# Contrast adjustment on one core: tiles of eight images in two slots among tiles of four in one

## The chip, the core and the metric

The kernel runs on one core of a Trainium2 chip. The metric is the device time of one execution in microseconds (us). The core's engines are named as the profile names them: PE (TensorE), DVE (VectorE), ACT (ScalarE), POOL (GpSimd) and SP (SyncE). Transfers between HBM and the on-chip memory run on 16 DMA engines; SP and ACT issue them, each on a queue of its own.

## What is computed

48 planes (16 images of 3 channels) of 512 × 512 float32 values, 1 MB each. This text calls a plane an image, as the change does. Each image is stretched about its own mean and clipped:

```python
x = rand(16, 3, 512, 512)          # float32, 50.3 MB
factor = 1.5
mean = np.mean(x, axis=(2, 3), keepdims=True)
return np.clip(mean + factor * (x - mean), 0, 1)
```

A value of the output depends on the whole image through its mean, so an image must have been read to its end before its first value can be written. With the mean folded in, an output value is factor · x + (1 − factor) · mean, clipped to 0 and 1.

## The kernel before

**Tiles.** An image is cut into 32 rows of 8,192 values (32 KB), one row to a partition, so a tile of 128 partitions holds four images, 4 MB. There are twelve tiles.

**The ring.** All data lives in one on-chip buffer, `ring`, of six slots of 32 KB per partition (line 66). Tile t uses slot t % 6. It is loaded there, changed in place and stored from there.

**Loads** are issued on SP (line 76). At the start five transfers fill the six slots: tile 0 in two parts (2,048 columns, then 6,144), tile 1, tiles 2 and 3 in one transfer, tiles 4 and 5 in one. After the computing of tile t, the load of tile t + 6 is issued (line 112); it waits until the store of tile t has landed, since it overwrites that slot. SP issues in order, so a load that waits holds up those behind it.

**Computing a tile** (lines 78 to 98). DVE adds up the first 4,352 columns of each row (line 81) while ACT adds up the other 3,840 (line 84; it writes a copy of them into `junk`, which nobody reads). Two matmuls on PE with the matrix `blockw` (lines 86, 87) add the partial sums of the 32 rows of an image, times (1 − factor)/pixels, and leave the result in `bias`, on each row of that image. The first waits for ACT's sum, the second for DVE's. Then DVE makes two passes over all 8,192 columns: times factor plus bias (line 91), and max with 0, min with 1 (line 94). `blockw` is made by POOL at the start (lines 61, 63): zeros, and four blocks of 32 × 32 with the weight.

**Stores** are issued on ACT after the second pass (line 101). The instructions of each engine stand in the order in which the program was written (`manual_schedule`): on ACT the store of tile t comes before the sum of tile t + 1, and on DVE the passes of tile t before the reduction of tile t + 1. Tile 0 is scaled and stored in two parts, of 2,048 and 6,144 columns.

Of the kernel before, what the change touches and what calls it, by code (L numbers as in the profile page):

```python
# [1 line left out]

# [4 lines left out]


P = 128  # L10
ROW = 8192
BUFS = 6
SHORT = 2048
FIRST = (SHORT, ROW - SHORT)
SUM = 4352


@with_exitstack
def kernel(
    ctx: ExitStack,  # L20
    tc: tile.TileContext,
    x: bass.AP,
    factor: float,
    out: bass.AP,
):

    nc = tc.nc
    f32 = mybir.dt.float32  # L30
    Alu = mybir.AluOpType
    Act = mybir.ActivationFunctionType

    B, C, H, W = x.shape
    n_img, n_pix = B * C, H * W
    ppi = n_pix // ROW
    per_tile = P // ppi
    n_tiles = n_img // per_tile
    assert ppi * ROW == n_pix and per_tile * n_tiles == n_img

    factor = float(factor)
    wconst = (1.0 - factor) / float(n_pix)

    x_f = x.rearrange("b c h w -> (b c h w)")
    out_f = out.rearrange("b c h w -> (b c h w)")

    def dram(ap, t, c0=0, c1=ROW):
        return bass.AP(tensor=ap.tensor, offset=t * P * ROW + c0, ap=[[ROW, P], [1, c1 - c0]])

    consts = ctx.enter_context(tc.tile_pool(name="consts", bufs=1))  # L50
    xpool = ctx.enter_context(tc.tile_pool(name="xpool", bufs=1))
    small = ctx.enter_context(tc.tile_pool(name="small", bufs=1))
    psum = ctx.enter_context(tc.tile_pool(name="psum", bufs=1, space=bass.MemoryType.PSUM))


    sums = small.tile([P, 2 * n_tiles], f32, name="sums")
    junk = small.tile([P, ROW - SUM], f32, name="junk")
    bias = psum.tile([P, n_tiles], f32, name="bias")

    blockw = consts.tile([P, P], f32, name="blockw")  # L60
    nc.gpsimd.memset(blockw, 0.0)  # L61
    for a in range(0, P, ppi):
        nc.gpsimd.memset(blockw[a : a + ppi, a : a + ppi], wconst)  # L63


    ring = xpool.tile([P, BUFS, ROW], f32, name="ring")

    def load(t, c0=0, c1=ROW, n=1):

        b = t % BUFS  # L70
        src = bass.AP(
            tensor=x_f.tensor,
            offset=t * P * ROW + c0,
            ap=[[ROW, P], [P * ROW, n], [1, c1 - c0]],
        )
        nc.sync.dma_start(out=ring[:, b : b + n, c0:c1], in_=src)  # L76

    def compute(t):
        xt = ring[:, t % BUFS, :]
        own = sums[:, 2 * t : 2 * t + 2]  # L80
        nc.vector.tensor_reduce(  # L81
            out=own[:, 0:1], in_=xt[:, 0:SUM], axis=mybir.AxisListType.X, op=Alu.add
        )
        nc.scalar.activation(out=junk, in_=xt[:, SUM:ROW], func=Act.Copy, accum_out=own[:, 1:2])  # L84
        shift = bias[:, t : t + 1]
        nc.tensor.matmul(shift, blockw, own[:, 1:2], start=True, stop=False)  # L86
        nc.tensor.matmul(shift, blockw, own[:, 0:1], start=False, stop=True)  # L87
        c = 0
        for n in FIRST if t == 0 else [ROW]:
            part = xt[:, c : c + n]  # L90
            nc.vector.tensor_scalar(  # L91
                out=part, in0=part, scalar1=factor, scalar2=shift, op0=Alu.mult, op1=Alu.add
            )
            nc.vector.tensor_scalar(  # L94
                out=part, in0=part, scalar1=0.0, scalar2=1.0, op0=Alu.max, op1=Alu.min
            )
            store(t, c, c + n)
            c += n

    def store(t, c0, c1):  # L100
        nc.scalar.dma_start(out=dram(out_f, t, c0, c1), in_=ring[:, t % BUFS, c0:c1])

    with tc.manual_schedule():
        load(0, c1=SHORT)
        load(0, c0=SHORT)
        load(1)
        load(2, n=2)
        load(4, n=2)
        for t in range(n_tiles):
            compute(t)  # L110
            if t + BUFS < n_tiles:
                load(t + BUFS)


# [1 line left out]
_INS = ['x', 'factor']  # L116
_OUTS = [((16, 3, 512, 512), 'float32')]

_NUMBERS = {'factor': 1.5}


# [26 lines left out]
```

## Time and profile before

| | us |
|---|---|
| median of the timed runs (three) | 239.27 |
| lowest and highest of them | 239.14, 239.34 |
| profiled execution, first to last instruction (the span) | 237.3 |
| DVE busy | 163.1 |
| ACT busy | 43.2 |
| PE busy | 14.1 |

The profile does not give a time for its own execution beside the span. The difference of its span from the median of the timed runs, 2.0 us, is what lies around the span.

How the lines are read. A line of groups or of the timeline names the program line (L81), the engine, the operation, output<-input, and partitions × elements. In the timeline the first two numbers are the start and the duration in us, and the bracket gives how long the engine had been idle and what ended that. SPq and ACTq stand for the issuing of transfers: the line says when a transfer is issued, not when it moves. In the DMA view, q1 is the queue that SP issues on (loads) and q10 the one that ACT issues on (stores); a queue's line gives its packets, their bytes in MB (of 1,000,000 bytes), and the time that the packets took, as a share of 16 engines over the window asked for.

The DMA rows of the page, with the size of one transfer and the median time from issue to landing:

| transfer | number | KB each | us from issue to landing |
|---|---|---|---|
| load, tile 0, first part | 1 | 1,024 | 4.8 |
| load, tile 0, second part | 1 | 3,072 | 11.7 |
| load, one tile | 7 | 4,096 | 49.7 |
| load, two tiles | 2 | 8,192 | 66.7 |
| store, tile 0, first part | 1 | 1,024 | 17.5 |
| store, tile 0, second part | 1 | 3,072 | 28.2 |
| store, one tile | 11 | 4,096 | 35.8 |

### The profile page before, as it was taken

What the parts mean: (1) busy time and instruction counts of PE and PEld (TensorE: products, weight loads), DVE (VectorE), ACT (ScalarE), POOL (GpSimd) and SP (SyncE); (2) the same over time, 40 slices, a digit from 0 to 9 for tenths busy, and PEclk for the clock granted to TensorE, in tenths of its full rate; (3) what the DMA queues carried; (4) which work ended last, traced back from release to release, by engine and by line L of the source; (5) the groups of instructions that cost most, each with busy time, mean ns of one, the idle gap of its engine ahead of it and who ended that gap; (6) DMA issues with size and microseconds to landing.
All of it is one profiled execution on the core that took longest, in us unless ns stands there. A gap on an engine that the chain in (4) does not pass through costs nothing.

```text
span 237.3 us, 285 instructions
## 1 busy us (share of the span) xinstructions
PE 14.1 (6%) x48; PEld 12.0 (5%) x48; DVE 163.1 (69%) x38; ACT 43.2 (18%) x25; POOL 0.9 (0%) x9
## 2 busy tenths in 40 slices
PE   0010010001010001010010100100100100010000
PEld 0010010001010001010010100100100100010000
DVE  0079989048989328999989898891892795687000
ACT  2050230041050023050320504101400500500000
POOL 1000000000000000000000000000000000000000
DMA  7999999999999999999999999999999999999996
GB/s 297 410 442 442 421 442 359 456 439 441 442 436 414 403 431 442 442 442 442 436 442 436 414 409 425 442 442 442 442 436 442 436 420 403 425 442 442 442 442 265
DMA packets 3712, 100.66 MB, mean 424 GB/s; under 512 B 384, under 2 KB 384, under 8 KB 384
## 3 DMA queue, kind: packets, MB, share of 16 engines
q1 hardware_dynamic: 1840, 50.33, 49.7%
q10 hardware_dynamic: 1872, 50.33, 49.2%
HBM read 50.33 MB, written 50.33 MB: 424 GB/s over the span
## 4 chain that ended last, share of the span: by engine, by line
DMA 57%; DVE 29%; another core or an unknown queue 3%; PE 1%; SPq 1%; issue 0%; DVEq 0%
DMA ring<-in_x_dram 41%; DMA out_dram<-ring 16%; DVE sums L81 10%; DVE ring L91 9%; DVE ring L94 9%; PE bias L87 1%; SPq L76 1%; DVEq L91 0%
## 5 line engine op out<-in xcount | busy, mean ns | idle before, releaser
L81 DVE TENSOR_REDUCE sums<-ring 128x1 f32<-128x4352 f32 x12 | 56.2, 4683 | 45.7 <-DMA ring<-in_x_dram 45.7
L84 ACT ACTIVATE junk<-ring 128x3840 f32<-128x3840 f32 x12 | 40.8, 3403 | 163.3 <-DMA ring<-in_x_dram 107.5
L91 DVE TENSOR_SCALAR ring<-ring,bias 128x8192 f32<-128x8192 f32 (+2 forms) x13 | 54.1, 4163 | 8.9 <-PE bias L87 7.4
L94 DVE TENSOR_SCALAR ring<-ring 128x8192 f32<-128x8192 f32 (+2 forms) x13 | 53.3, 4099 | 0.4
L86 PE MATMUL bias<-sums,blockw 128*128 128x1 f32 x24 | 7.0, 361 | 190.8 <-ACT junk L84 190.8
L86 PEld LDWEIGHTS bias<-sums,blockw 128*128 128x128 f32 x24 | 6.0, 312 | 191.7 <-ACT junk L84 175.2
L87 PE MATMUL bias<-sums,blockw 128*128 128x1 f32 x24 | 7.0, 363 | 4.3 <-DVE sums L81 3.9
L87 PEld LDWEIGHTS bias<-sums,blockw 128*128 128x128 f32 x24 | 6.0, 311 | 5.3 <-DVE sums L81 5.0
L84 ACT ACTIVATION_READ_ACCUMULATOR junk<-ring 128x1 f32 x12 | 2.2, 186 | 0.0
L84 ACT ACT_TABLE_LOAD x1 | 1.3, 1283 | 0.7 <-PEq L129 0.7
L63 POOL MEMSET blockw<- 32x32 f32 x4 | 0.5, 117 | 0.2
L61 POOL MEMSET blockw<- 128x128 f32 x1 | 0.2, 204 | 0.3 <-POOLq L129 0.3
L129 POOL MEMSET const-bfloat16-1.0<- 128x1 bf16 x1 | 0.1, 111 | 0.0
L129 POOL MEMSET const-uint8-127<- 128x1 uint8 x1 | 0.1, 111 | 0.0
L129 POOL MEMSET const-float32-1.0<- 128x1 f32 x1 | 0.1, 108 | 0.0
L129 POOL MEMSET const-float32-0.0<- 128x1 f32 x1 | 0.1, 103 | 0.2 <-issue 0.2
## 6 DMA issues: line engine op xcount, KB each, us to landing
out_dram<-ring ACTq DMA_DIRECT2D x11, 4096.0 KB, 35.8
ring<-in_x_dram SPq DMA_DIRECT2D x7, 4096.0 KB, 49.7
ring<-in_x_dram SPq DMA_DIRECT2D x2, 8192.0 KB, 66.7
ring<-in_x_dram SPq DMA_DIRECT2D x1, 3072.0 KB, 11.7
out_dram<-ring ACTq DMA_DIRECT2D x1, 3072.0 KB, 28.2
ring<-in_x_dram SPq DMA_DIRECT2D x1, 1024.0 KB, 4.8
out_dram<-ring ACTq DMA_DIRECT2D x1, 1024.0 KB, 17.5
```

What stands on the lines that cost most here:

```text
L61: nc.gpsimd.memset(blockw, 0.0)
L63: nc.gpsimd.memset(blockw[a : a + ppi, a : a + ppi], wconst)
L76: nc.sync.dma_start(out=ring[:, b : b + n, c0:c1], in_=src)
L81: nc.vector.tensor_reduce(out=own[:, 0:1], in_=xt[:, 0:SUM], axis=mybir.AxisListType.X, op=Alu.add)
L84: nc.scalar.activation(out=junk, in_=xt[:, SUM:ROW], func=Act.Copy, accum_out=own[:, 1:2])
L86: nc.tensor.matmul(shift, blockw, own[:, 1:2], start=True, stop=False)
L87: nc.tensor.matmul(shift, blockw, own[:, 0:1], start=False, stop=True)
L91: nc.vector.tensor_scalar(out=part, in0=part, scalar1=factor, scalar2=shift, op0=Alu.mult, op1=Alu.add)
L94: nc.vector.tensor_scalar(out=part, in0=part, scalar1=0.0, scalar2=1.0, op0=Alu.max, op1=Alu.min)
L129: nc = _bacc.Bacc("TRN2", target_bir_lowering=False, num_devices=1)
```

## The change

The program is written for tiles of two sizes. `PLAN` lists, for each of eight tiles, its first slot and its number of slots: (0, 1), (1, 2), (3, 2), (5, 1), and the same again. A one-slot tile is as before: four images in rows of 32 KB. A two-slot tile holds eight images, each in 16 rows of 16,384 values (64 KB), and a row lies in two neighbouring slots of its partition.

- `load` and `store` move one tile each, 4 or 8 MB. The transfers of two tiles at once are gone: at the start tile 0 is loaded in two parts, then tiles 1, 2 and 3. Tile t + 4 takes the place of tile t and is loaded after its store.
- The sums: for one slot DVE adds up 3,840 columns and ACT 2,176 twice; for two slots DVE adds up 7,552 and ACT 2,944 three times. There is one matmul for each partial sum, ACT's first and DVE's last: three for one slot, four for two.
- The two passes of DVE run over 8,192 or 16,384 columns. Tile 0 is still cut in two.
- There are two block matrices, for 32 and for 16 rows to an image, each made on POOL by a memset and two affine selects.

```diff
-ROW = 8192
-BUFS = 6
+UNIT = 8192
+SLOTS = 6
 SHORT = 2048
-FIRST = (SHORT, ROW - SHORT)
-SUM = 4352
+PLAN = ((0, 1), (1, 2), (3, 2), (5, 1)) * 2
+
+ACT = {1: (2176, 2176), 2: (2944, 2944, 2944)}
...
+    def dram(ap, t, c0, c1):
+        row = UNIT * PLAN[t][1]
+        return bass.AP(tensor=ap.tensor, offset=start[t] + c0, ap=[[row, P], [1, c1 - c0]])
...
-    blockw = consts.tile([P, P], f32, name="blockw")
-    nc.gpsimd.memset(blockw, 0.0)
-    for a in range(0, P, ppi):
-        nc.gpsimd.memset(blockw[a : a + ppi, a : a + ppi], wconst)
+    block = {}
+    for w in sorted({w for _, w in PLAN}):
+        rows = n_pix // (UNIT * w)
+        m = consts.tile([P, P], f32, name=f"block{w}")
+        nc.gpsimd.memset(m, wconst)
+        v = m.rearrange("p (g j) -> p g j", j=rows)
+        nc.gpsimd.affine_select(
+            out=v, in_=v, pattern=[[-rows, P // rows], [0, rows]], compare_op=Alu.is_ge,
+            fill=0.0, base=0, channel_multiplier=1,
+        )
+        nc.gpsimd.affine_select(
+            out=v, in_=v, pattern=[[rows, P // rows], [0, rows]], compare_op=Alu.is_ge,
+            fill=0.0, base=rows - 1, channel_multiplier=-1,
+        )
+        block[w] = m
...
+    def cols(t, c0, c1):
+        a = PLAN[t][0] * UNIT
+        return ring[:, a + c0 : a + c1]
+
+    def load(t, c0=0, c1=None):
+        c1 = UNIT * PLAN[t][1] if c1 is None else c1
+        nc.sync.dma_start(out=cols(t, c0, c1), in_=dram(x_f, t, c0, c1))
+
+    def store(t, c0, c1):
+        nc.scalar.dma_start(out=dram(out_f, t, c0, c1), in_=cols(t, c0, c1))
...
+        vec = row - sum(ACT[w])
         nc.vector.tensor_reduce(
-            out=own[:, 0:1], in_=xt[:, 0:SUM], axis=mybir.AxisListType.X, op=Alu.add
+            out=own[:, 0:1], in_=cols(t, 0, vec), axis=mybir.AxisListType.X, op=Alu.add
         )
-        nc.scalar.activation(out=junk, in_=xt[:, SUM:ROW], func=Act.Copy, accum_out=own[:, 1:2])
+        a = vec
+        for i, n in enumerate(ACT[w], 1):
+            nc.scalar.activation(
+                out=junk[:, 0:n], in_=cols(t, a, a + n), func=Act.Copy,
+                accum_out=own[:, i : i + 1],
+            )
+            a += n
         shift = bias[:, t : t + 1]
-        nc.tensor.matmul(shift, blockw, own[:, 1:2], start=True, stop=False)
-        nc.tensor.matmul(shift, blockw, own[:, 0:1], start=False, stop=True)
+        for i in range(1, len(ACT[w]) + 1):
+            nc.tensor.matmul(shift, block[w], own[:, i : i + 1], start=i == 1, stop=False)
+        nc.tensor.matmul(shift, block[w], own[:, 0:1], start=False, stop=True)
...
+    held, after = {}, {}
+    for t, (s, w) in enumerate(PLAN):
+        before = [held[k] for k in range(s, s + w) if k in held]
+        after.setdefault(max(before, default=-1), []).append(t)
+        held.update({k: t for k in range(s, s + w)})

     with tc.manual_schedule():
-        load(0, c1=SHORT)
-        load(0, c0=SHORT)
-        load(1)
-        load(2, n=2)
-        load(4, n=2)
-        for t in range(n_tiles):
+        load(0, 0, SHORT)
+        load(0, SHORT)
+        for t in after[-1][1:]:
+            load(t)
+        for t in range(len(PLAN)):
             compute(t)
-            if t + BUFS < n_tiles:
-                load(t + BUFS)
+            for n in after.get(t, ()):
+                load(n)
```

More of the change, by code (lines that the diff above doesn't have):

```diff
@@ L34 @@
     B, C, H, W = x.shape
[L35 to L39, printed above, removed]
+    n_pix = H * W
+    assert P * UNIT * sum(w for _, w in PLAN) == B * C * n_pix
     factor = float(factor)
@@ L45 @@
     out_f = out.rearrange("b c h w -> (b c h w)")
-    def dram(ap, t, c0=0, c1=ROW):
-        return bass.AP(tensor=ap.tensor, offset=t * P * ROW + c0, ap=[[ROW, P], [1, c1 - c0]])
+    start, begin = [], 0
+    for _, w in PLAN:
+        start.append(begin)
+        begin += P * UNIT * w
+    def dram(ap, t, c0, c1):
+        row = UNIT * PLAN[t][1]
+        return bass.AP(tensor=ap.tensor, offset=start[t] + c0, ap=[[row, P], [1, c1 - c0]])
     consts = ctx.enter_context(tc.tile_pool(name="consts", bufs=1))
@@ L53 @@
     psum = ctx.enter_context(tc.tile_pool(name="psum", bufs=1, space=bass.MemoryType.PSUM))
-    sums = small.tile([P, 2 * n_tiles], f32, name="sums")
-    junk = small.tile([P, ROW - SUM], f32, name="junk")
-    bias = psum.tile([P, n_tiles], f32, name="bias")
-    blockw = consts.tile([P, P], f32, name="blockw")
-    nc.gpsimd.memset(blockw, 0.0)
-    for a in range(0, P, ppi):
-        nc.gpsimd.memset(blockw[a : a + ppi, a : a + ppi], wconst)
-    ring = xpool.tile([P, BUFS, ROW], f32, name="ring")
@@ L68, in load @@
[L68 to L74, printed above, removed]
-        )
-        nc.sync.dma_start(out=ring[:, b : b + n, c0:c1], in_=src)
+    sums = small.tile([P, 4 * len(PLAN)], f32, name="sums")
+    junk = small.tile([P, max(map(max, ACT.values()))], f32, name="junk")
+    bias = psum.tile([P, len(PLAN)], f32, name="bias")
+    block = {}
[7 more added lines that the diff above has]
+            fill=0.0, base=0, channel_multiplier=1,
+        )
+        nc.gpsimd.affine_select(
[3 more added lines that the diff above has]
+        block[w] = m
@@ L78, in compute @@
+    ring = xpool.tile([P, SLOTS * UNIT], f32, name="ring")
+    def cols(t, c0, c1):
[6 more added lines that the diff above has]
+        nc.scalar.dma_start(out=dram(out_f, t, c0, c1), in_=cols(t, c0, c1))
     def compute(t):
-        xt = ring[:, t % BUFS, :]
-        own = sums[:, 2 * t : 2 * t + 2]
+        w = PLAN[t][1]
+        row = UNIT * w
+        own = sums[:, 4 * t : 4 * t + 4]
+        vec = row - sum(ACT[w])
@@ L85, in compute @@
         shift = bias[:, t : t + 1]
-        nc.tensor.matmul(shift, blockw, own[:, 1:2], start=True, stop=False)
-        nc.tensor.matmul(shift, blockw, own[:, 0:1], start=False, stop=True)
+        for i in range(1, len(ACT[w]) + 1):
+            nc.tensor.matmul(shift, block[w], own[:, i : i + 1], start=i == 1, stop=False)
+        nc.tensor.matmul(shift, block[w], own[:, 0:1], start=False, stop=True)
         c = 0
-        for n in FIRST if t == 0 else [ROW]:
-            part = xt[:, c : c + n]
+        for n in (SHORT, row - SHORT) if t == 0 else (row,):
+            part = cols(t, c, c + n)
@@ L98, in compute @@
             c += n
-    def store(t, c0, c1):
-        nc.scalar.dma_start(out=dram(out_f, t, c0, c1), in_=ring[:, t % BUFS, c0:c1])
-    with tc.manual_schedule():
-        load(0, c1=SHORT)
-        load(0, c0=SHORT)
-        load(1)
-        load(2, n=2)
-        load(4, n=2)
-        for t in range(n_tiles):
+    held, after = {}, {}
[3 more added lines that the diff above has]
+        held.update({k: t for k in range(s, s + w)})
+    with tc.manual_schedule():
+        load(0, 0, SHORT)
[3 more added lines that the diff above has]
+        for t in range(len(PLAN)):
             compute(t)
-            if t + BUFS < n_tiles:
-                load(t + BUFS)
+            for n in after.get(t, ()):
+                load(n)
 _INS = ['x', 'factor']
```

## The prediction

> **What bounds the kernel now.** I read the page's DMA parts first, because the file is little but traffic: 50.33 MB in, 50.33 MB out.
>
> ```profile
> span 237.3 us, 285 instructions
> PE 14.1 (6%) x48; PEld 12.0 (5%) x48; DVE 163.1 (69%) x38; ACT 43.2 (18%) x25; POOL 0.9 (0%) x9
> DMA packets 3712, 100.66 MB, mean 424 GB/s; under 512 B 384, under 2 KB 384, under 8 KB 384
> q1 hardware_dynamic: 1840, 50.33, 49.7%
> q10 hardware_dynamic: 1872, 50.33, 49.2%
> ```
>
> The two queues' packets fill 49.7 + 49.2 = 98.9% of the span on all 16 DMA engines: 234.7 of 237.3 us. What is left, 2.6 us, is the start (the first load is issued at 0.74) and the end. So the engines that move data never wait; VectorE at 69% does. The packet counts say what a packet is: 1,536 rows of 32 KB each way, 128 more where tile 0 is cut in two, and 16 small ones for each of 24 transfers (the 384 under 512 B): 2 × 1,664 + 384 = 3,712. One row, one packet.
>
> Next the DMA view in two windows: one in which only stores run (208 to 235 us), then one in which stores of 8 KB rows meet loads of 32 KB rows (25.5 to 36.5 us).
>
> ```profile
> DMA packets 386, 11.60 MB, mean 430 GB/s; under 512 B 32, under 2 KB 32, under 8 KB 32
> q10 hardware_dynamic: 386, 11.60, 99.5%
> ```
> ```profile
> DMA packets 233, 4.69 MB, mean 426 GB/s; under 512 B 0, under 2 KB 0, under 8 KB 0
> q1 hardware_dynamic: 113, 3.70, 79.6%
> q10 hardware_dynamic: 120, 0.98, 21.1%
> ```
>
> One queue alone fills the engines. Two share by packets, not by bytes: 113 packets against 120, but 3.70 MB against 0.98. Whoever has the longer packets gets more of the bandwidth; this decides below.
>
> Last the timeline of the final tile: its load landed at 203.7, the store is issued 14.4 us later, and it lands only 18.3 us after that (DMA view), where its own 4 MB need 9.7: a backlog of stores covers the computing.
>
> ```profile
> 203.76 4.69 DVE L81 TENSOR_REDUCE sums<-ring 128x1 f32<-128x4352 f32 x1 [4.98 <-DMA ring<-in_x_dram]
> 203.82 3.40 ACT L84 ACTIVATE junk<-ring 128x3840 f32<-128x3840 f32 x1 [15.86 <-DMA ring<-in_x_dram]
> ...
> 209.18 4.49 DVE L91 TENSOR_SCALAR ring<-ring,bias 128x8192 f32<-128x8192 f32 x1 [0.74 <-PE bias L87]
> 213.71 4.43 DVE L94 TENSOR_SCALAR ring<-ring 128x8192 f32<-128x8192 f32 x1
> 218.17 0.34 ACTq L101 DMA_DIRECT2D out_dram<-ring  x1
> ```
>
> So the time is start + bytes at a fixed rate + packet costs + any moment in which both queues are empty. The profiled span is 237.3, the median of the timed runs 239.27; the 2.0 around the span I leave as it is and add differences to 239.27.
>
> **The change, part by part.** *Packets.* In the trace's packet records an 8, 24 and 32 KB packet takes 309, 912 and 1,213 ns, and neighbours on one engine start 4 ns before the last ends: 305, 908, 1,209. Eight KB cost 301 ns each; 3.7 ns is left for the packet itself. The new tiles have 1,024 rows each way plus 128 for the cut one, where there were 1,664: 1,024 packets fewer, 64 per engine, 64 × 3.7 = 0.24 us. Transfers fall from 24 to 18; their closing packets take 9 ns on each engine: 0.05. Gain 0.29 us. Taken with the recorded 309 and 1,213 instead (7.6 ns fixed) it is 0.54; if packets overlap fully, 0. I take 0.29, since starts are what adds up. A 64 KB packet, which no row shows, would be 2,414 ns by this line.
>
> *Compute per tile.* Two-slot tiles: L91 and L94 grow from 4,491 and 4,427 to 8,758 and 8,694 ns (slope from the 2,048 rows: 1,291 and 1,227), 17.5 together. The reduction of 7,552 columns: at most 4,683 × 7,552/4,352 = 8.1. ScalarE's three sums of 2,944: between 2.6 (in proportion to 3,403 for 3,840) and 3.4 each, and 0.19 to read each out: 8.4 to 10.8; I take 8.6, near the proportion. Then two matmul steps of 0.6 that must follow the last sum. From landing to store: 27.8 us (29.6 at worst), against 14.4. One-slot tiles: 14.9, since ScalarE (two sums, about 4.4) now ends after VectorE (4.2). In all 4 × 27.8 + 4 × 14.9 = 171 against 12 × 14.3 = 172: off the path as long as the queues have work. ACT issues the store of tile t before the sums of t+1, as now. More matmuls (28 for 24) cost nothing in themselves: PE is 6% busy.
>
> *Block matrices.* Five memsets (0.20 and 4 of 0.12) become two memsets and four affine selects, which no row shows. From 0.2 each to 2.6 each they end before PE's first matmul at 16.5, their only reader: nothing. Were they later still, tile 0's store would be, with loads queued until 75.
>
> *Loads, stores and waits.* The same 24 MB are issued at the start, now one after the other: tile 1's 8 MB land near 32 (4 MB landed at 22.5), tile 2's near 55. SP's load of tile t+4 waits for the store of tile t, all 8 MB of it for t = 1 and 2; later loads stand behind it on SP. Nothing starves while the other queue has packets, so I walked the queues by hand: alternate packets, 1.21 us for 32 KB, 2.41 for 64, compute as above. Tile: load lands / store issued / store lands (us):
>
> - 1: 32 / 61 / 96; 2: 55 / 88 / 131; 3: 75 / 103 / 160
> - 4: 104 / 120 / 183; 5: 140 / 169 / 206
> - 6: 170 / 198 / 225; 7: 191 / 212.5 / 235
>
> The same walk over the kernel before puts its last load at 203.6 (trace 203.7). At no time are both queues empty. The narrow place is the store of tile 6: with tile 5's gone at 206, only stores 6 and 7 remain. It is issued at 198; from issue to first packet takes 1.0 us (first load: 0.74 to 1.75) to 3.7 (first store, against loads: 20.9 to 24.6). Room: 206 − 198 − (1.0 to 3.7) = 4 to 7 us, more than the 1.8 by which ScalarE may be slower.
>
> That a 64 KB row is one packet is taken from 8, 24 and 32 KB rows, which all are. The Trainium skill, page "DMA: Bandwidth & Descriptors", section "Why a DMA increments its semaphore by 16 and not by 1", says that one descriptor moves one contiguous run and speaks of cutting only rows beyond 64 KiB; no run here shows such a row. Against the change speaks the same page's section "Latency and other measured facts": rows 512 KiB apart moved at 207 GB/s where 214 was full. The rows here lie 32 KB apart at an even rate and would lie 64 KB apart; if that whole 3% fell on the two thirds of the bytes in long rows, my estimate from that page would be 239.0 + 4.7 = 243.7.
>
> **Sum:** 239.27 − 0.24 − 0.05 = 238.98, say 239.0: minus 0.12%. A measurement of this kernel can tell about 0.2% (0.48 us) from no change.
>
> **Rivals.** *Slower: tile 6's store comes too late.* If a 64 KB row travels as two packets of 32 KB, loads lose their two to one over the 32 KB stores 3 and 4. When load 6 lands, 44 MB (of 1,024 KB) have been loaded and S stored; 40 − S MB (load 7 and the stores up to tile 5) are left to cover tile 6's computing, at 2.42 us per MB. Whole rows: landing at 170 means S = 25, cover 36 us, need 27.8 + 1.0 to 3.7. Cut rows: the walk lands load 6 at 180, S = 29, cover 26 us: 2.8 to 5.5 us with both queues empty, so 242.0 to 244.7 with 0.05 for the closing packets off. It decides when tile 6's store is issued after 202 to 205. For it: no packet over 32 KB has been seen. Against: every row so far was one packet. *Slower rate* for long rows: as bound without a row, zero to the 2% between the two windows shown (430 and 426 GB/s are 1% apart; twice that) on 155 us: up to 3. Against: the engines keep one rate alone and mixed. *Faster:* the fixed cost is what the records say, 0.54 or more: 238.7. Against: the starts.
>
> **How the numbers follow.** Whole rows, no gap 0.60: 238.75 to 239.3, its chance of passing 0.2% small (0.04). Larger fixed cost 0.11. Late store, whatever makes it late 0.18. Slower rate 0.11. Faster 0.04 + 0.11 = 0.15; same 0.56; slower 0.18 + 0.11 = 0.29. The range takes the first two, the milder half of the late store and most of the slower rate: 238.6 to 243.0.
>
> **What would show it.** Right: 2,304 + 288 = 2,592 packets, the two queues at about 98.9%, a 64 KB packet near 2,414 ns, tile 6's store issued by 200, no slice below 400 GB/s but the first and last. Wrong: 3,616 packets (rows cut) with a dip at 206; or whole rows and the same dip, if the chain of tiles 5 and 6 ends after 203; or whole rows of 2,450 ns and more.

## The result, and the profile after

| | before | changed |
|---|---|---|
| median of 14 runs each, us | 239.27 | 241.3 |
| lowest and highest | 239.12, 239.46 | 239.38, 244.18 |
| profiled execution, span | 237.3 | 241.7 |

The changed kernel is slower: ratio 1.0049, 95% interval 1.0032 to 1.0066. Ratios, here and below, leave out runs more than 1.5% above the fastest of their kernel, here four (243.3 to 244.2, the profiled one among them), so for a scattered kernel the ratio is below that of the medians, here 1.0085. The spread is the first thing to see. Before, 14 runs agree within 0.34 us; now they lie between 239.4 and 244.2, all at one granted clock.

The page of the changed kernel, its head, the GB/s row of the 40 slices, and the queues:

```profile
span 241.7 us, 286 instructions
...
GB/s 296 399 521 347 557 412 401 377 433 385 445 499 418 380 450 412 445 423 494 369 499 369 494 380 488 369 434 439 423 428 429 466 477 380 499 369 499 358 374 27
DMA packets 2592, 100.66 MB, mean 417 GB/s; under 512 B 288, under 2 KB 288, under 8 KB 288
...
q1 hardware_dynamic: 1296, 50.33, 48.9%
q10 hardware_dynamic: 1296, 50.33, 48.2%
```

2,592 packets: every row went as one packet, the 64 KB rows too. But the queues fill 97.1% of 16 engines, not 98.9%: 7.0 us of 241.7 are idle, against 2.6 before. The windows at the end of the changed kernel show where (columns: stretch, length, busy time of five engines, all idle here, granted clock, DMA share, GB/s):

```profile
230.00:235.00 5.00, 0.00 (x0) 0.00 (x0) 0.00 (x0) 0.00 (x0) 0.00 (x0) 1.00 0.97 419
235.00:236.00 1.00, 0.00 (x0) 0.00 (x0) 0.00 (x0) 0.00 (x0) 0.00 (x0) 1.00 0.23 98
236.00:238.00 2.00, 0.00 (x0) 0.00 (x0) 0.00 (x0) 0.00 (x0) 0.00 (x0) 1.00 0.15 66
238.00:240.00 2.00, 0.00 (x0) 0.00 (x0) 0.00 (x0) 0.00 (x0) 0.00 (x0) 1.00 0.04 16
```

From 236 to 240 a few engines are still moving data; 0.15 is about 2 to 3 of 16. The packet records name them. Each transfer leaves one small closing packet on every engine, and its end tells when that engine was through (us; the last column has the other three engines, sorted by time):

| closing packet of | 13 engines | the other three |
|---|---|---|
| store, tile 0, first part | 46.3–46.7 | 43.9, 44.0, 44.3 |
| load, tile 2 | 56.8–57.2 | 58.8, 58.8, 59.1 |
| load, tile 3 | 78.3–78.7 | 81.7, 81.8, 82.1 |
| load, tile 4 | 107.3–107.7 | 111.4, 111.5, 112.9 |
| load, tile 6 | 171.3–171.7 | 174.9, 175.1, 177.2 |
| store, tile 5 | 206.4–206.8 | 208.8, 209.0, 211.0 |
| store, tile 7, the end | 235.4–235.8 | 237.8, 238.0, 240.0 |

Thirteen engines end at 235.4 to 235.8, where before's ended at 235.5 to 236.1. Three end 2.0 to 4.6 us later, and the kernel waits for the last. They part at one place. The first store is issued at 20.82 and its first packets run about 3.6 us later, at 24.4, while a load packet of 64 KB ends on every engine between about 24.2 and 24.5. The DMA view of the changed kernel from 24 to 26 us:

```profile
DMA packets 19, 1.07 MB, mean 537 GB/s; under 512 B 0, under 2 KB 0, under 8 KB 0
...
q1 hardware_dynamic: 16, 1.05, 125.4%
q10 hardware_dynamic: 3, 0.02, 2.9%
```

Sixteen load packets and three store packets. Three engines had the store's packet in time and took it now. The other thirteen took the next load packet first and their store packet at 26.6 and later. From there the three are one load packet behind with their loads and one store packet ahead. That alone loses nothing, since the same bytes are to be moved. But packets on them then took longer. Followed packet by packet back from 240.0, the latest engine has 5.2 us over the usual durations (2,418 ns for 64 KB, 1,213 for 32) in 10 packets; the largest are 64 KB loads at 48.0 (+1.10) and 115.4 (+1.40) and a 32 KB load at 97.5 (+0.94). The first engine in step to end has 0.9. With 0.4 from a later start, 5.2 − 0.9 + 0.4 = 4.7: the 4.6 by which it ends later. The other two late engines, followed with the known order of an engine's transfers as a guide, also lead back to a store packet at 24.4; their packets are 3.1 and 3.2 us over the usual durations, those of the thirteen 0.9 to 1.1.

The timeline of the changed kernel, tiles 5 to 7, shows what the late engines do to tile 6:

```profile
175.64 0.34 ACTq L93 DMA_DIRECT2D out_dram<-ring  x1
...
177.59 8.02 DVE L100 TENSOR_REDUCE sums<-ring 128x1 f32<-128x7552 f32 x1 [1.99 <-DMA ring<-in_x_dram]
...
187.14 8.76 DVE L117 TENSOR_SCALAR ring<-ring,bias 128x16384 f32<-128x16384 f32 x1 [1.53 <-PE bias L113]
...
195.93 8.69 DVE L120 TENSOR_SCALAR ring<-ring 128x16384 f32<-128x16384 f32 x1
...
204.66 0.34 ACTq L93 DMA_DIRECT2D out_dram<-ring  x1
...
219.50 0.34 ACTq L93 DMA_DIRECT2D out_dram<-ring  x1
```

The reduction waits for the last engine of the load (177.2), not for the thirteen (171.7). With the thirteen alone it would still have waited until 175.6 for VectorE, which was at work on tile 5: that tile's load, too, was complete only with its latest engine, at 148.2 (142.3 to 142.7 on the thirteen). So the store of tile 6 leaves at 204.66 instead of the 198 foretold. Its first packets still come before the thirteen run dry at 206.8 (at 206.4 the trace has them go on without a pause), so no gap follows.

### The profile page after: what moved, and what is told of

Same layout as the page of the kernel before. It is cut to its first block, busy times and chain, and to the rows that moved or that the text cites. A ratio compares the mean times of both kernels' runs of the same rounds, so it can differ in the third digit from the quotient of the medians.

```text
span 241.7 us, 286 instructions
## 1 busy us (share of the span) xinstructions
PE 15.1 (6%) x56; PEld 13.4 (6%) x56; DVE 154.2 (64%) x26; ACT 51.2 (21%) x41; POOL 1.7 (1%) x10
## 2 busy tenths in 40 slices
DMA packets 2592, 100.66 MB, mean 417 GB/s; under 512 B 288, under 2 KB 288, under 8 KB 288
## 4 chain that ended last, share of the span: by engine, by line
DMA 50%; DVE 25%; ACT 12%; PE 2%; issue 1%; SPq 0%; ACTq 0%; DVEq 0%
DMA ring<-in_x_dram 31%; DMA out_dram<-ring 19%; DVE ring L117 13%; DVE ring L120 13%; ACT junk L105 12%; PE bias L112 1%; PE bias L113 1%; SPq L90 0%; ACTq L93 0%; DVEq L117 0%; ACTq L105 0%
## 5 line engine op out<-in xcount | busy, mean ns | idle before, releaser
L100 DVE TENSOR_REDUCE sums<-ring 128x1 f32<-128x3840 f32 (+1 forms) x8 | 48.7, 6084 | 52.2 <-DMA ring<-in_x_dram 52.2
L105 ACT ACTIVATE junk<-ring 128x2944 f32<-128x2944 f32 (+1 forms) x20 | 48.0, 2401 | 157.4 <-DMA ring<-in_x_dram 99.6
L117 DVE TENSOR_SCALAR ring<-ring,bias 128x16384 f32<-128x16384 f32 (+3 forms) x9 | 53.2, 5913 | 12.7 <-PE bias L113 12.7
L120 DVE TENSOR_SCALAR ring<-ring 128x16384 f32<-128x16384 f32 (+3 forms) x9 | 52.6, 5849 | 0.3
L112 PE MATMUL bias<-sums,block 128*128 128x1 f32 x40 | 11.7, 361 | 195.3 <-ACT junk L105 195.3
L112 PEld LDWEIGHTS bias<-sums,block 128*128 128x128 f32 x40 | 10.0, 311 | 196.9 <-ACT junk L105 163.2
L113 PE MATMUL bias<-sums,block 128*128 128x1 f32 x16 | 4.5, 352 | 0.0
L113 PEld LDWEIGHTS bias<-sums,block 128*128 128x128 f32 x16 | 4.4, 333 | 0.0
L105 ACT ACTIVATION_READ_ACCUMULATOR junk<-ring 128x1 f32 x20 | 3.7, 187 | 0.0
L72 POOL TENSOR_SCALAR_AFFINE_SELECT block<-block 128x128 f32<-128x128 f32 x2 | 0.6, 329 | 0.0
L76 POOL TENSOR_SCALAR_AFFINE_SELECT block<-block 128x128 f32<-128x128 f32 x2 | 0.6, 328 | 0.0
## 6 DMA issues: line engine op xcount, KB each, us to landing
out_dram<-ring ACTq DMA_DIRECT2D x1, 1024.0 KB, 26.2
```

The costliest lines, as they stand in the source:

```text
L72: nc.gpsimd.affine_select(out=v, in_=v, pattern=[[-rows, P // rows], [0, rows]], compare_op=Alu.is_ge, fill=0.0, base=0, channel_multiplier=1,
L76: nc.gpsimd.affine_select(out=v, in_=v, pattern=[[rows, P // rows], [0, rows]], compare_op=Alu.is_ge, fill=0.0, base=rows - 1, channel_mul ...
L100: nc.vector.tensor_reduce(out=own[:, 0:1], in_=cols(t, 0, vec), axis=mybir.AxisListType.X, op=Alu.add)
L105: nc.scalar.activation(out=junk[:, 0:n], in_=cols(t, a, a + n), func=Act.Copy, accum_out=own[:, i : i + 1],)
L112: nc.tensor.matmul(shift, block[w], own[:, i : i + 1], start=i == 1, stop=False)
L113: nc.tensor.matmul(shift, block[w], own[:, 0:1], start=False, stop=True)
```

## Experiments

Theories: **the race**: the changed kernel's extra time comes from engines that fall out of step where the first store meets the border of a 64 KB load packet; move the store by half a packet and it goes, by a whole packet and it returns. **Long packets**: 64 KB rows cost in themselves (in the load, the store, or in both). **The short first pieces**: 8 and 24 KB store packets beside 64 KB loads are the cost. All comparisons are with the kernel before, run beside them; its median was 239.23 to 239.26 in the three groups of runs. Medians are of all runs. The changed kernel itself was not run again in these groups.

### The first store 1.1 us later

ScalarE adds up fewer columns of a one-slot tile and VectorE more, so the first store is issued at 21.90 instead of 20.82. The shares change in all four one-slot tiles, not in tile 0 alone.

```diff
-ACT = {1: (2176, 2176), 2: (2944, 2944, 2944)}
+ACT = {1: (1408, 1408), 2: (2944, 2944, 2944)}
```

> The changed kernel with one edit: in one-slot tiles ScalarE adds up 1,408 columns twice instead of 2,176, VectorE the other 5,376. This moves tile 0's first store from 20.8 to about 21.9 us and nothing else that matters. In the changed kernel three of the 16 DMA engines took their first store packet at 24.3 to 24.5 us, between two 64 KB load packets, the other 13 one packet later, and the three ended 2.2 to 4.5 us after the others. Theory A (out of step): the store reaches the engines just as their load packets end, so chance splits them, and an engine that is out of step with the others loses time at later changes of transfer. With the store 1.1 us later it falls inside the packet from 24.2 to 26.7 on all engines: all in step, last store packets within 0.6 us of each other, runs within 0.4 us of each other at 239.3 to 239.7. Theory B (the mixed order of 4 and 8 MB transfers does it, wherever the first store falls): engines end up to 4.5 us apart as now, runs between 239.4 and 244.2.

Measured: 238.97 us (238.80 to 239.13 in 11 runs), below the 239.3 to 239.7 that was expected, ratio 0.9985 (0.9976 to 0.9993). The spread is gone. The DMA view of this kernel from 24 to 26 us, then from 26.2 to 28.4:

```profile
DMA packets 16, 1.05 MB, mean 524 GB/s; under 512 B 0, under 2 KB 0, under 8 KB 0
...
q1 hardware_dynamic: 16, 1.05, 129.2%
```
```profile
q1 hardware_dynamic: 16, 1.05, 111.6%
q10 hardware_dynamic: 16, 0.13, 14.0%
```

No engine takes a store packet in the first window, all 16 take one in the second. They stay together to the end (235.4 to 235.8). Its timeline has the reduction of tile 6 and its store 5.5 us earlier than the changed kernel:

```profile
172.13 8.02 DVE L100 TENSOR_REDUCE sums<-ring 128x1 f32<-128x7552 f32 x1 [1.95 <-DMA ring<-in_x_dram]
...
199.20 0.34 ACTq L93 DMA_DIRECT2D out_dram<-ring  x1
```

So the extra time is not that of long packets: they are all still there. And 238.97 is the sum that the prediction made, 238.98.

### Half a packet, a whole one, one and a half

The same edit with (768, 768) and (192, 192): the first store at 23.14 and at 24.44.

```diff
-ACT = {1: (2176, 2176), 2: (2944, 2944, 2944)}
+ACT = {1: (768, 768), 2: (2944, 2944, 2944)}
```

> As the run with 1,408 columns, but ScalarE adds up 768 columns twice in one-slot tiles, VectorE 6,656. Tile 0's first store should be issued near 23.2 us: 2.4 us, one 64 KB packet, after the changed kernel's 20.8. Theory A (the first store meets a packet boundary): the store again reaches the engines as a load packet ends, now near 26.7, so chance splits them again: last store packets 1 to 5 us apart in most runs, runs spread over 1 to 4 us, median 239.6 to 241.5. Rival (any later first store cures it, because more loads are through, or the changed share of the sums did it): steady as with 1,408, 238.8 to 239.2.

```diff
-ACT = {1: (2176, 2176), 2: (2944, 2944, 2944)}
+ACT = {1: (192, 192), 2: (2944, 2944, 2944)}
```

> ScalarE adds up 192 columns twice in one-slot tiles, VectorE 7,808; tile 0's first store near 24.4 us, one and a half packets after the changed kernel's. Theory A: inside a packet again (26.7 to 29.1) on all engines: in step, last store packets within 0.6 us, runs within 0.4 us at 238.8 to 239.2. Rival (the share of the sums, or luck in the run with 1,408): no return to steady runs, or slower by what the longer reductions cost (VectorE 4 us more per one-slot tile).

Measured: at 23.14, 242.12 us (239.51 to 244.38 in 12 runs), ratio 1.0073 (1.0044 to 1.0101): the spread is back, with a median above the 239.6 to 241.5 expected. At 24.44, 238.89, ratio 0.9982 (0.9973 to 0.9991): ten runs from 238.82 to 239.01, and an eleventh at 244.5, which was not profiled and stays unexplained. The two kernels were run beside each other. The DMA view of the first of the two from 26.2 to 28.4 us:

```profile
q1 hardware_dynamic: 16, 1.05, 115.8%
q10 hardware_dynamic: 10, 0.08, 8.8%
```

Ten engines take a store packet there and six do not. The execution profiled here was one of the good ones (239.58), so being divided does not always cost; it makes the time a matter of chance.

### The first store moved in another way

In the two kernels above VectorE's load changes with the store's time. Here the sums stay as in the changed kernel, and the first part of tile 0 gets another width: its store is issued at 19.76 (1,024 columns) or at 21.97 (3,072).

```diff
-SHORT = 2048
+SHORT = 1024
```

> The changed kernel with SHORT = 1024: tile 0 is cut at 1,024 columns, its first store issued near 19.8 us, 1.1 earlier than the changed kernel's. The sums stay as they are. Theory A (the first store must not meet a packet boundary of the 64 KB loads; those end near 21.8 and 24.3, and a store is ready 3.5 us after its issue): ready at 23.3, inside a packet: in step, last store packets within 0.6 us, runs 238.8 to 239.2. Rival (a later first store, or fewer columns for ScalarE, is what cured it): spread as in the changed kernel, 239.4 to 244.

```diff
-SHORT = 2048
+SHORT = 3072
```

> SHORT = 3072: first store near 21.9 us, as in the run with 1,408 columns, by another way. Theory A: ready at 25.4, inside a packet: in step, runs 238.8 to 239.2. Rival (the share of the sums): spread as in the changed kernel.

Measured: 239.17 (239.05 to 239.43 in 11 runs), ratio 0.9997 (0.9987 to 1.0006), steady but with four runs above the 239.2 expected, and 239.00 (238.89 to 239.18 in 11), ratio 0.9993 (0.9984 to 1.0002). In the DMA view of the first, from 24 to 26 us, all sixteen engines take a store packet; in that of the second none does, and all do from 26.2 to 28.4:

```profile
q1 hardware_dynamic: 16, 1.05, 120.9%
q10 hardware_dynamic: 16, 0.07, 8.0%
```
```profile
q1 hardware_dynamic: 16, 1.05, 111.6%
q10 hardware_dynamic: 16, 0.20, 20.9%
```

Ordered by the time of the first store's issue, the six kernels are: 19.76 steady, 20.82 scattered, 21.90 and 21.97 steady, 23.14 scattered, 24.44 steady but for one run. The two scattered ones are 2.32 us apart; a 64 KB load packet comes every 2.41.

### Transfers of 32 KB rows for the two-slot tiles

Tiles and computing stay as changed, but a two-slot tile's transfers go as two of 8,192 columns: loads and stores, stores alone, loads alone. The load's edit (the store's is the same):

```diff
-        nc.sync.dma_start(out=cols(t, c0, c1), in_=dram(x_f, t, c0, c1))
+        for c in range(c0, c1, UNIT):
+            e = min(c + UNIT, c1)
+            nc.sync.dma_start(out=cols(t, c, e), in_=dram(x_f, t, c, e))
```

Both cut:

> The changed kernel, but each transfer of a two-slot tile goes as two of 32 KB pieces of its rows, loads and stores: no packet over 32 KB, the same tiles and order. Theory A: a step is 1.2 us and its later losses small, as in the kernel before (one engine 1.3 us behind, no loss at the end): engines end within 1.5 us of each other, runs within 0.5 us. The walk of the prediction for cut rows then holds: load 6 lands near 180, store 6 is issued near 207 to 208, both queues are empty for 2.8 to 5.5 us from 206, time 242.0 to 244.7 in every run. Theory B: the same gap and engines 2 to 5 us apart on top, runs spread over 4 us.

Stores cut, loads whole:

> The changed kernel, but stores of two-slot tiles go as two transfers of 32 KB pieces; loads keep rows of 64 KB. By the walk loads have two packets' bytes to one, no gap at tile 6. Theory A: the first store still meets 64 KB load packets at 24.3, so engines can still fall out of step by 2.4 us; if being out of step is all it takes, runs spread as in the changed kernel (239.4 to 244); if the losses need long packets on both queues, engines end within 1.5 us and runs at 239.3 to 240.3. Theory B: spread as in the changed kernel.

Loads cut, stores whole:

> The changed kernel, but loads of two-slot tiles go as two transfers of 32 KB pieces; stores keep rows of 64 KB. Theory A: at the first store a step is only 1.2 us, as in the kernel before, so engines end within 1.5 us of each other. By the walk loads now get one packet's bytes to two of the stores: load 5 lands near 154, store 6 is issued near 208, both queues are empty for about 4 us from 206: 241.5 to 244.5, steady within 0.7 us. Theory B: engines 2 to 5 us apart on top of the gap.

| rows | us (lowest, highest, runs) | ratio, 95% |
|---|---|---|
| loads 32, stores 32 KB | 239.46 (239.10, 239.94, 11) | 1.0008 (1.0000 to 1.0017) |
| loads 64, stores 32 | 239.78 (239.21, 240.60, 12) | 1.0025 (1.0014 to 1.0035) |
| loads 32, stores 64 | 247.7 (244.40, 251.14, 6) | 1.0238 (1.0213 to 1.0262) |

*Both cut* was to show the rival of the prediction in which loads lose their two to one and the store of tile 6 comes 2.8 to 5.5 us too late. It did not. Its timeline:

```profile
203.10 4.15 DVE L104 TENSOR_REDUCE sums<-ring 128x1 f32<-128x3840 f32 x1
203.22 1.07 ACTq L97 DMA_DIRECT2D out_dram<-ring  x2
```

The store of tile 6 leaves at 203.22 and that of tile 5 is gone at 206.4 to 207.5: no gap. The edit does more than cut packets. Each half is waited for by itself, so a reduction starts on the first half (tile 1's at 27.2), and loads leave earlier. A row that is cut but waited for as a whole was not tried, so that rival's price stays unmeasured.

*Stores cut* is divided at the start as the changed kernel is: 6 of 16 engines take the first store early. Yet the profiled execution, one of its quicker (239.32), ends within 235.6 to 236.3, 0.7 us apart, and its slowest run is at 240.60 where the changed kernel's is at 244.18. So being divided cost less with stores of 32 KB. It is not gone: the median is 0.55 us above that of the kernel before.

*Loads cut* is the dearest of the three, above the 241.5 to 244.5 expected and far from steady. Six engines fall behind, in two steps: by 2.5 to 3 us with the load of tile 3, by 5 to 6 with that of tile 4 (112.1–112.4 on ten engines, 117.5–118.6 on six). Here the late store does come. The load of tile 5 is complete at 155.1 to 155.4 on ten engines and at 160.8 to 162.9 on six; tiles 5 and 6 are then computed one after the other, and the store of tile 6 is issued at 217.79, 54.9 us after the latest. From 155.4 the same 54.9 would have ended at 210.3 (worked out, not run), just ahead of the end of tile 5's store, which was gone at 210.6 to 213.7; with 1.0 us and more from issue to first packet a gap of some 0.7 us would have stayed on the ten engines. The windows of this kernel:

```profile
211.00:214.00 3.00, 0.00 (x0) 0.00 (x0) 3.00 (x1) 0.00 (x0) 0.00 (x0) 1.00 0.05 22
214.00:219.00 5.00, 0.00 (x0) 0.00 (x0) 5.00 (x2) 0.77 (x1) 0.00 (x0) 1.00 0.49 210
```

Almost no data moves from 211 to 214 while VectorE is still at work on tile 6. This is the "both queues empty" of the prediction, and by that sum most of it comes from engines that are out of step: the load that the computing waits for is as late as its latest engine.

### Stores cut and moved

```diff
-ACT = {1: (2176, 2176), 2: (2944, 2944, 2944)}
+ACT = {1: (1408, 1408), 2: (2944, 2944, 2944)}
...
-        nc.scalar.dma_start(out=dram(out_f, t, c0, c1), in_=cols(t, c0, c1))
+        for c in range(c0, c1, UNIT):
+            e = min(c + UNIT, c1)
+            nc.scalar.dma_start(out=dram(out_f, t, c, e), in_=cols(t, c, e))
```

> Both: stores of two-slot tiles as two transfers of 32 KB pieces, and 1,408 columns. With cut stores six engines were out of step and lost under 1 us; with cut loads and 64 KB stores six lost up to 8. So what costs is a 64 KB store packet out of step. Theory A: in step and without the long stores: 239.0 to 239.3, no run over 239.6; 32 more packets per engine and four more transfers than with 1,408 alone cost 32 x 3.7 ns + 4 x 9 = 0.15 us. Rival: the two cures are not independent, runs up to 240.6 as with cut stores alone.

Measured: 239.38 (238.84 to 239.93 in 11 runs), ratio 1.0003 (0.9993 to 1.0013): above the 239.0 to 239.3 expected, with one run over 239.6. The engines are together at the start, but five end the load of tile 6 at 173.0 to 173.6 us, the other eleven at 171.2 to 171.8, and the end lies between 235.4 and 236.5. The start is not the only place at which engines can part.

### Tile 0 in one piece

If the short first pieces were the cost, one 32 KB piece should take it away: in the changed kernel, and in the kernel before. In the first the sums were changed too; the store is issued at 29.34.

```diff
-ACT = {1: (2176, 2176), 2: (2944, 2944, 2944)}
+ACT = {1: (1024, 1024), 2: (2944, 2944, 2944)}
...
-        for n in (SHORT, row - SHORT) if t == 0 else (row,):
+        for n in (row,):
```

> ScalarE adds up 1,024 columns twice in one-slot tiles (VectorE 6,144), and tile 0 is scaled and stored in one piece of 8,192 columns, issued near 29.2 us. In the runs so far the load packets beside tile 0's short stores took longer than 2,418 ns on every engine: +0.15 us at 24.2, +0.31 at 29.8 and +0.58 at 46.5 (8 KB pieces change to 24 KB), 1.05 us in all. Theory A adds: the first store falls inside a packet (31.5 to 33.9), so all are in step. If the short pieces cause the long packets, most of the 1.05 goes: 238.1 to 238.5, steady. Rival (any first store costs this, whatever its pieces): 238.8 to 239.2.

```diff
-        for n in FIRST if t == 0 else [ROW]:
+        for n in [ROW]:
```

> The kernel before with tile 0 scaled and stored in one piece (issued near 28). Its load packets beside the short stores were longer by 0.28, 0.2 and 0.44 us too, 0.85 per engine. If the short pieces cause this: 238.5 to 238.9, with packets of 32 KB alone. Rival: 239.1 to 239.4, no change, or slower by the 7 us that the first store comes later, if that starves a queue (it should not: loads are queued to 50 us).

Both miss. The changed kernel gives 255.5 (254.51 to 261.97 in 6 runs), 1.0649 (1.0632 to 1.0665); the kernel before 240.45 (239.50 to 241.81 in 12), 1.0048 (1.0033 to 1.0062). In the first all engines are together until 61.5. There the store of tile 0 and the load of tile 2, eight packets each on every engine and begun together, end at the same moment, and two engines take the next transfers in the other order. On those two the eight 64 KB store packets of tile 1, beside 32 KB loads, then take 0.4 to 1.4 us longer each; the load of tile 3 lands there at 98.2, on the others at 88, and that of tile 7 at 220.9, on the others at 187.6 to 190.7. The GB/s row of this kernel:

```profile
GB/s 289 537 330 496 475 269 496 485 341 423 413 454 485 392 387 429 454 361 444 423 454 351 413 470 418 454 372 418 434 284 351 382 434 207 52 496 444 382 413 248
```

Slices 34 and 35 (207 and 52) are a gap ahead of a late store again. In the second, whose slowest run was profiled, one engine's load packet at 30.7 takes 2.16 us longer and that engine ends at 238.4, the others at 235.8 to 236.7. So the tiles of the kernel before are exposed too; that its own 14 even runs are owed to the time of its first store is likely, but not shown. The short pieces are not the cost: on engines in step, the load packets up to 61 us are over their usual durations by 0.8 to 1.2 us in sum with tile 0 in one piece, and by 0.4 to 1.1 us with the short pieces.

## Why the prediction was wrong, and where it was right

**Bound and packets: right.** One row, one packet: 2,592. A 64 KB packet took 2,418 ns and its neighbour starts 4 ns before its end: the 2,414 of the line through 8, 24 and 32 KB. The gain of 0.29 us agrees with three of the four kernels in step: 238.97, 239.00 and 238.89 against 238.98, two of them with intervals that exclude no change. The fourth, with the first part of 1,024 columns, gave 239.17, ratio 0.9997, and shows no gain. So the sum is supported, its size not shown.

**Rate: no loss.** The rival of a slower rate, and the 3% for far rows that the Trainium skill's page "DMA: Bandwidth & Descriptors", section "Latency and other measured facts", gives at a larger distance, would need 2,450 ns and more per packet: 2,418 is less than two packets of 32 KB (2 × 1,213 = 2,426). Rows 64 KB apart cost nothing here.

**Compute per tile: right.** The groups of the changed kernel by shape (count, then busy us and mean ns, then idle time ahead and its releaser):

```profile
L117 DVE TENSOR_SCALAR ring<-ring,bias 128x16384 f32<-128x16384 f32 x4 | 35.0, 8758 | 6.6 <-PE bias L113 6.6
...
L100 DVE TENSOR_REDUCE sums<-ring 128x1 f32<-128x7552 f32 x4 | 32.1, 8018 | 29.1 <-DMA ring<-in_x_dram 29.1
...
L105 ACT ACTIVATE junk<-ring 128x2944 f32<-128x2944 f32 x12 | 31.9, 2657 | 87.8 <-DMA ring<-in_x_dram 68.5 <-DVE ring L120 19.1
```

8,758 to the nanosecond, 8,018 under the bound of 8.1, ScalarE at 2,657, near the proportion. From the start of the reduction to the store: 204.66 − 177.59 = 27.1, and from landing (177.2) 27.5, against 27.8. Two slips in the working change nothing that was measured: the worst case would be 27.8 − 8.6 + 10.8 = 30.0, not 29.6, and the cover with cut rows 11 × 2.42 = 26.6, not 26. The affine selects took 0.33 us each, inside 0.2 to 2.6.

**The walk of the queues: right for an engine, wrong for sixteen.** Thirteen engines keep to it closely: stores of tiles 1, 2, 3, 4, 5 at 96.6, 131.6, 160.6, 183.6, 206.6 (walk: 96, 131, 160, 183, 206), the load of tile 6 at 171.5 (170). The step that failed is "Nothing starves while the other queue has packets, so I walked the queues by hand: alternate packets". It took the 16 engines as one. Each of them alternates by itself, and whether the first store packet comes before or after a load packet was decided engine by engine. The trace of the kernel before already held this: its first store packet, read as 24.6, is that of one engine, and the other fifteen take theirs at 25.3 to 25.8. No case of the prediction had engines out of step, so none had its price: in the profiled execution three engines end 2.0 to 4.6 us after the others, and the median is 241.3 where the first shifted kernel, in step, has 238.97.

**Luck in the range.** 241.3 lies inside the 238.6 to 243.0 that was stated, but for other reasons: the upper part of the range was there for a late store and a slower rate, and in the changed kernel neither was the cost.

**The late store: half right.** The store of tile 6 was issued at 204.66, inside the 202 to 205 from which it was said to decide, since a tile is complete only with its latest engine: 177.2, not 171.7. In the changed kernel the room was used up without a gap; with the loads cut, and with tile 0 whole, there was one.

**A sign that was badly chosen:** "no slice below 400 GB/s". The first shifted kernel, with all engines in step, has slices of 353 and 530. A slice is 5.94 us; sixteen 64 KB packets that end together, two or three times in a slice, are 2 × 1.05/5.94 = 353 and 3 × 1.05/5.94 = 530. That is what a view shows that counts a packet where it ends.

**What stays open:** why packets of an engine that is out of step take longer, and why sometimes 1.4 us and sometimes nothing; in the kernel at 23.14 the profiled execution was divided and lost nothing. The changed kernel has one profile, of a run at 243.36; whether the engines of its quicker runs were divided too is not shown. Shown are the place where engines part in that execution, that moving the first store by half a packet removes the spread in all runs but one and by a whole one brings it back, and that the spread is smaller with 32 KB stores.

**The better version** is one of the shifted kernels, (1408, 1408) or (192, 192): ratios 0.9985 and 0.9982 to the kernel before. It gains 0.3 us and may keep a risk: (192, 192) had the one run at 244.5.

## To carry to other kernels

A transfer is as late as the latest of its 16 engines, so a queue model with one server for all of them says nothing of their spread: look for the closing packets by engine before trusting it. Here longer rows saved a few nanoseconds for each packet, by the prediction's estimate, and raised the price of an engine that goes another way. When a kernel's runs suddenly scatter, look for a transfer that begins just where another queue's packet ends, and try moving it by half a packet.

## What the hardware showed unasked

- The time depends on the moment of a single store, and the two scattered cases lie about one packet apart: steady at 239.2, 239.0 and 238.9 us with the store at 19.8, 21.9 and 24.4, but for one run at 244.5; scattered up to 244.4 with it at 20.8 and 23.1.
- A packet is not of constant length: on engines in step up to 0.66 us is added to a packet where stores first meet loads in the changed kernel, and up to 0.97 with tile 0 whole; on an engine out of step up to 1.40 and 1.58 in the same two kernels, and 2.16 in the kernel before with tile 0 whole.
- Loads of 32 KB rows with stores of 64 KB cost 2.4% (3.5% by the median of all six runs), the reverse 0.25%: in these two kernels it mattered more which queue had the long packets than how many there were.
